# Running log-sum-exp: loads and stores put into the DMA queue in twos instead of by turns

## The chip, the cores and the metric

The kernel runs on one core of a Trainium2 chip. The metric is the device time of one execution in microseconds (us), the median of several runs. The profile is of one execution of its own; its times are counted from the first instruction.

## What is computed

The input is a float32 array of 4 batches, 4096 rows and 4128 columns. For each batch and column the output is the running log-sum-exp down the rows:

```python
out[:, 0, :] = x[:, 0, :]
for t in range(1, S):
    mx = np.maximum(out[:, t - 1, :], x[:, t, :])
    out[:, t, :] = mx + np.log(np.exp(out[:, t - 1, :] - mx) + np.exp(x[:, t, :] - mx))
```

This is the logarithm of the prefix sum of exp(x). Every element is read from HBM once and written back once: 270.5 MB each way.

## The kernel before

**Steps.** A step is 384 rows of one batch, all 4128 columns: 128 partitions with R = 3 neighbouring rows each (6192 KB). 4096 rows make 10 such steps and one of 256 rows (R = 2, 4128 KB). The short step is the first one in batch 0 and the last one in batches 1, 2 and 3. There are 44 steps, numbered 0 to 43 here; the short ones are 0, 21, 32 and 43. One DMA loads a whole step (line L127, `load`), one DMA stores it (L130, `store`). Both are issued on SyncE's queue (SP), which works through its instructions in the order of the program and stops at each until its semaphores allow it. In this text "load n" and "store n" are the transfers of step n.

**Buffers.** The pool `xpool` has 4 buffers of a whole step (`bufs = 4`). exp is written as fp16 into the buffer itself and the logarithm is written back over it as float32, so one buffer holds a step from its load to the end of its store. Load n+4 reuses the buffer of step n and waits until store n has landed (and TensorE has read the buffer).

**Compute.** A step is cut into 4 chunks of 1024 columns (the last one has 1056). For each chunk ScalarE (ACT) takes exp of all rows (L142), TensorE (PE) adds up the rows in PSUM by multiplying with triangular 0/1 matrices, with a carry from the step before (L92, L96), ScalarE takes the logarithm of the first row (L175, `Ln`), TensorE adds the second row, and so on, so a chunk has three stages. The last 32 columns have a PSUM tile of their own (L180). VectorE (DVE) copies the last row's sum into the carry as two fp16 parts (L106, L107).

**Order of the work.** The order is written out by hand (`manual_schedule`). Iteration g of the main loop does the stage of the third row of chunk g-2, of the second row of chunk g-1 and of the first row of chunk g; then exp of chunk g+2; then the matmuls of chunk g+1. ScalarE works strictly in this order. So exp of the first three chunks of step n+1 stands ahead of the last `Ln` of step n: step n can't be finished, and store n not be issued, before load n+1 has landed.

**Order of the transfers.** Loads 0 to 3 are issued at the start. After that a finished step issues its store and then, from the second step on, one load, three steps ahead:

```python
k.t.store()
if bufs <= stored + ahead < len(steps):
    steps[stored + ahead].load()
stored += 1
```

So SP's program is load 0 to 3, store 0, store 1, load 4, store 2, load 5, store 3, load 6, and so on; at the end load 42, store 40, load 43, stores 41, 42, 43. This order is a program order: where `store()` stands in the Python loop fixes what SP has to get past before it, and a store waits for ScalarE's count of the last `Ln` of its own step.

Of the kernel before, what the change touches and what calls it, by code (L numbers as in the profile page):

```python
# [49 lines left out]
def kernel(  # L50
# [23 lines left out]
    bufs = 4  # L74
# [110 lines left out]
    steps = []  # L185
# [9 lines left out]
        assert row == S  # L195

    chunks = [Chunk(s, c) for s in steps for c in range(n_main)]
    ahead = bufs - 1
    for s in steps[:bufs]:
        s.load()  # L200
    stored = 0
    chunks[0].exp()
    chunks[1].exp()
    chunks[0].head()
    for g in range(len(chunks) + R - 1):
        for d in range(R - 1, -1, -1):
            if 0 <= g - d < len(chunks) and d < chunks[g - d].t.r:
                k = chunks[g - d]
                k.stage(d)
                if k.c == last and d + 1 == k.t.r:  # L210
                    k.t.store()
                    if bufs <= stored + ahead < len(steps):
                        steps[stored + ahead].load()
                    stored += 1
        if g + 2 < len(chunks):
            chunks[g + 2].exp()
        if g + 1 < len(chunks):
            chunks[g + 1].head()
# [30 lines left out]
```

## Time and profile before

| | before |
|---|---|
| median of 3 runs | 1262.8 us (1262.75 to 1262.93) |
| span of the profiled execution, first to last instruction | 1261.0 us |
| busy: PE, DVE, ACT | 690.7 (55%), 451.4 (36%), 947.0 us (75%) |
| DMA: bytes, mean rate, mean busy share in the 40 slices | 541.46 MB, 429 GB/s, 90% or more in all but the last |
| transfers on SP's queue | 44 loads and 44 stores |
| load, issue to landing (median) | 42.2 us |
| store, issue to landing (median) | 28.1 us |

The page of the profile lists busy time by engine, then the span in 40 slices, the DMA queues, the chain of work that ended last, and the groups of instructions and of transfers. A transfer is cut over 16 DMA engines, each of which takes its part (8 rows of a step's 128) and then goes on to its part of the next transfer in the queue. A transfer has landed when the last of the 16 has reported. The profiled execution has no time of its own beside the span; the median of the runs is 1.8 us above it, and that is taken as what lies around the span.

### The profile page before, as it was taken

The page shows a single profiled execution, that of the slowest core. Times are in us where ns is not written, and L with a number is a line of the kernel's source. Part 1 is how long each engine was busy: PE and PEld are TensorE (multiplying, and loading weights), DVE is VectorE, ACT ScalarE, POOL GpSimd, SP SyncE. Part 2 cuts the span into 40 slices and gives each one's busy share as a digit, 9 for nine tenths or more (in the row PEclk, how much of TensorE's full clock was granted, in tenths as well). Part 3 has the DMA queues.
Part 4 walks back from the last instruction along what each step waited for, and adds up shares of the span by engine and source line. Part 5 has one row for each costly group of instructions (what it writes and reads, how often), then busy time and mean ns, then how long its engine had stood idle before and what let it go on. Part 6 is the DMA issues. An engine that isn't in the chain of part 4 may idle for free.

```text
span 1261.0 us, 6165 instructions
## 1 busy us (share of the span) xinstructions
PE 690.7 (55%) x2268; PEld 236.3 (19%) x2268; DVE 451.4 (36%) x445; ACT 947.0 (75%) x733; POOL 2.2 (0%) x13
## 2 busy tenths in 40 slices
PE   3666545565565555555346655555534755555562
PEld 1222111121121111111112221211211211111120
DVE  2443333333333333334424333333442433333344
ACT  5997777777777777778569777777866977777784
POOL 0000000000000000000000000000000000000000
PEclk9987787877777777878778777777777778787776
DMA  9999999999999999999999999999999999999998
GB/s 411 411 443 428 432 429 437 431 431 434 437 429 431 431 439 431 434 427 434 436 431 433 434 431 438 430 434 432 435 431 433 437 430 434 433 434 431 433 420 348
DMA packets 12702, 541.46 MB, mean 429 GB/s; under 512 B 1408, under 2 KB 1408, under 8 KB 1408
## 3 DMA queue, kind: packets, MB, share of 16 engines
q1 hardware_dynamic: 12672, 541.07, 99.4%
q8 instruction: 18, 0.29, 0.1%
q14 instruction: 12, 0.10, 0.0%
HBM read 270.53 MB, written 270.53 MB: 429 GB/s over the span
## 4 chain that ended last, share of the span: by engine, by line
DMA 72%; ACT 19%; PE 5%; issue 2%; DVE 1%; SPq 0%; ACTq 0%
DMA xt<-in_x_dram 67%; ACT xt L142 10%; ACT xt L175 9%; DMA out_dram<-xt 5%; PE pt L96 3%; PE pt L92 2%; DVE carry L106 0%; DVE carry L107 0%; ACT xt L180 0%; SPq L130 0%; ACTq L244 0%; SPq L127 0%; ACTq L142 0%; PE qt L92 0%
## 5 line engine op out<-in xcount | busy, mean ns | idle before, releaser
L142 ACT ACTIVATE xt<-xt 128x3072 f16<-128x3072 f32 (+3 forms) x176 | 478.2, 2717 | 247.9 <-DMA xt<-in_x_dram 247.8
L175 ACT ACTIVATE xt<-pt 128x1024 f32<-128x1024 f32 x512 | 487.3, 1029 | 2.5 <-PE pt L96 0.7
L106 DVE CAST carry<-pt 32x1024 f16<-32x1024 f32 x176 | 216.5, 1230 | 760.9 <-ACT xt L175 760.7
L92 PE MATMUL pt<-xt,ident 128*128 128x512 f16 x176 | 76.6, 435 | 493.7 <-ACT xt L175 493.7
L96 PE MATMUL pt<-xt,ident 128*128 128x512 f16 x496 | 203.7, 477 | 35.4 <-ACT xt L175 34.7
L107 DVE TENSOR_TENSOR carry<-pt,carry 32x1024 f16<-32x1024 f32 x176 | 215.8, 1226 | 6.1
L96 PE MATMUL pt<-xt,excl 128*128 128x512 f16 x496 | 187.6, 496 | 0.0
L96 PEld LDWEIGHTS <-ident 128*128 128x128 f16 x496 | 51.0, 103 | 655.0 <-issue 641.3
L92 PE MATMUL pt<-xt,incl 128*128 128x512 f16 x176 | 92.2, 524 | 23.5 <-ACT xt L142 15.1
L92 PE MATMUL pt<-xt,excl 128*128 128x512 f16 x176 | 93.4, 531 | 0.0
L96 PE MATMUL pt<-xt,incl 128*128 128x512 f16 x176 | 92.9, 528 | 0.0
L96 PEld LDWEIGHTS <-excl 128*128 128x128 f16 x536 | 66.6, 124 | 104.1 <-issue 79.5
L92 PE MATMUL pt<-carry,pick 128*128 128x512 f16 x160 | 72.0, 450 | 0.0
L96 PE MATMUL pt<-carry,pick 128*128 128x512 f16 x160 | 68.5, 428 | 0.0
L180 ACT ACTIVATE xt<-qt 128x96 f32<-128x96 f32 (+1 forms) x44 | 10.9, 248 | 46.3 <-PE pt L96 46.3
L92 PEld LDWEIGHTS <-incl 128*128 128x128 f16 x220 | 22.6, 103 | 118.0 <-DVE carry L107 95.3
L92 PEld LDWEIGHTS <-excl 128*128 128x128 f16 x220 | 26.8, 122 | 36.8 <-issue 27.9
L96 PEld LDWEIGHTS <-incl 128*128 128x128 f16 x260 | 27.8, 115 | 10.9 <-issue 4.8
L92 PEld LDWEIGHTS <-pick 128*128 128x128 f16 x200 | 22.9, 114 | 30.4 <-issue 20.4
L96 PEld LDWEIGHTS <-pick 128*128 128x128 f16 x160 | 18.4, 115 | 28.6 <-issue 17.2
L92 PEld LDWEIGHTS <-ident 128*128 128x128 f16 x176 | 19.2, 109 | 22.7 <-issue 12.8
L106 DVE CAST carry_t<-qt 32x32 f16<-32x32 f32 x44 | 8.7, 197 | 26.0 <-ACT xt L180 25.8
(21 smaller groups left out, 56.5 us busy)
## 6 DMA issues: line engine op xcount, KB each, us to landing
xt<-in_x_dram SPq DMA_DIRECT2D x40, 6192.0 KB, 42.2
out_dram<-xt SPq DMA_DIRECT2D x40, 6192.0 KB, 28.1
xt<-in_x_dram SPq DMA_DIRECT2D x4, 4128.0 KB, 37.3
out_dram<-xt SPq DMA_DIRECT2D x4, 4128.0 KB, 29.6
```

The source lines that it names most:

```text
L92: nc.tensor.matmul(pt, lhsT=w, rhs=rhs, start=start, stop=stop, skip_group_check=True)
L96: pe.add_instruction(mybir.InstMatmult(name=nc.get_next_instruction_name(), ins=[pe.lower_ap(rhs), pe.lower_ap(w, for_matmul_weights=True) ...
L106: nc.vector.tensor_copy(cr[HI:HI + 32, :], pt[HI:HI + 32])
L107: nc.vector.tensor_tensor(out=cr[LO:LO + 32, :], in0=pt[HI:HI + 32], in1=cr[HI:HI + 32, :], op=mybir.AluOpType.subtract,)
L142: nc.scalar.activation(self.t.half[:, :, 2 * c0:2 * c0 + w], self.t.xt[:, :, c0:c0 + w], ACT.Exp,)
L175: nc.scalar.activation(t.xt[:, j, c * CH:(c + 1) * CH], pt, ACT.Ln)
L180: nc.scalar.activation(t.xt[:, :, t0:D], self.qt, ACT.Ln)
```

## The change

Steps are no longer stored one at a time. A counter `done` counts finished steps; at every second one (`group = bufs // 2` is 2) the two stores are written into the program, and after them the loads of the two steps that reuse their buffers.

```diff
-    ahead = bufs - 1
+    group = bufs // 2
     for s in steps[:bufs]:
         s.load()
-    stored = 0
+    stored = done = 0
...
                 if k.c == last and d + 1 == k.t.r:
-                    k.t.store()
-                    if bufs <= stored + ahead < len(steps):
-                        steps[stored + ahead].load()
-                    stored += 1
+                    done += 1
+                    if done % group == 0 or done == len(steps):
+                        for s in steps[stored:done]:
+                            s.store()
+                        for s in steps[stored + bufs:done + bufs]:
+                            s.load()
+                        stored = done
```

SP's program becomes load 0 to 3, store 0, store 1, load 4, load 5, store 2, store 3, load 6, load 7, and so on; at the end load 42, load 43, stores 40, 41, 42, 43. The number and size of the transfers, the buffers, and the instruction streams of PE, DVE, ACT and POOL stay as they are. The built programs give each store the same ScalarE count to wait for in both kernels (51 for store 2, 68 for store 3: each waits for its own step alone), and each load the same landed store and the same TensorE count.

## Prediction

> **What bounds the kernel now.** I read the page first, for engines and DMA.
>
> ```profile
> span 1261.0 us, 6165 instructions
> PE 690.7 (55%) x2268; PEld 236.3 (19%) x2268; DVE 451.4 (36%) x445; ACT 947.0 (75%) x733; POOL 2.2 (0%) x13
> DMA  9999999999999999999999999999999999999998
> GB/s 411 411 443 428 432 429 437 431 431 434 437 429 431 431 439 431 434 427 434 436 431 433 434 431 438 430 434 432 435 431 433 437 430 434 433 434 431 433 420 348
> xt<-in_x_dram SPq DMA_DIRECT2D x40, 6192.0 KB, 42.2
> out_dram<-xt SPq DMA_DIRECT2D x40, 6192.0 KB, 28.1
> ```
>
> No compute engine is busy over 75%; the DMA engines are full from end to end at a flat rate. In the trace's packets nearly every one of 49536 bytes takes 1829 ns on its engine, in load and store alike; an engine takes 8 of them per transfer, 14.63 us. With 40 long and 4 short steps (two thirds as long), in and out, that is 2 x 14.63 x (40 + 4 x 2/3) = 1248.5 us per engine; with 1.8 us before the first packet and 0.9 us from last packet to landing, 1251.2 us. The last store lands at 1260.2 us, so only some 9 us are left above the bare engine time. Now where each engine waits:
>
> ```profile
> ACT xt L142 <- DMA xt<-in_x_dram: 247.8, 42, 11.8
> SPq L130 <- ACT xt L175: 1174.4, 44, 30.0
> SPq L127 <- DMA out_dram<-xt: 18.4, 5, 4.9
> ```
>
> ScalarE waits for a load in nearly every step; SP waits for the step's last `Ln` before a store, and hardly ever for a store to land before a load. The chain of waits and SP's timeline show the loop:
>
> ```profile
> 1124.20 42.49 DMA xt<-in_x_dram
> 1166.71 2.76 ACT xt L142
> ...
> 1182.54 0.33 SPq L130
> ```
> ```profile
> 1153.19 0.33 SPq L130 DMA_DIRECT2D out_dram<-xt  x1
> 1153.61 0.38 SPq L127 DMA_DIRECT2D xt<-in_x_dram  x1
> 1182.54 0.33 SPq L130 DMA_DIRECT2D out_dram<-xt  x1
> ```
>
> Load 41 lands at 1166.7, ScalarE starts exp of step 41, and 15.83 us after that start SP issues store 40 (1182.54). This distance is 15.83 us in nearly all long steps. The chain makes it look like a loop of latency, but the 42 us of a load are 28 us of queue and 14.6 us of work: the transfers in front of it keep the engines full. ScalarE's own work for a long step is 23.25 us (1137.36 to 1166.71, less 6.10 us of waiting):
>
> ```profile
> 1137.36 2.76 ACT L142 ACTIVATE xt<-xt 128x3072 f16<-128x3072 f32 x1 [6.16 <-DMA xt<-in_x_dram]
> 1166.71 2.76 ACT L142 ACTIVATE xt<-xt 128x3072 f16<-128x3072 f32 x1 [6.10 <-DMA xt<-in_x_dram]
> ```
>
> against 29.25 us for its two transfers. So the limit is the DMA engines; the question is whether the new order lets them run dry.
>
> **The change, part by part.** Nothing is added or taken away in transfers, bytes or compute. What moves is SP's order.
>
> *Changes of direction.* Before, load and store alternate, so there are about 80 changes; after, half of them. What does one cost? From the landing events (last of 16 engines): load after load at the start 14.60 and 14.62 us apart; load after store 14.55 and store after load 14.69 through most of the run, mean 14.62; the short store 43 after store 42 9.76, against 9.81 for a short store behind a load and 9.68 for a short load behind a store. The two means agree within 0.02 us with unmixed neighbours, and the 0.14 us between load and store comes and goes with the completion. Price of a change of direction 0.00 to 0.02 us; 40 fewer save 0 to 1 us. I take 0.
>
> *Loads later, stores earlier in the queue.* Take four transfers of a pair as 58.5 us, and let load 2m+2 land at 0. Load 2m+3 follows at 14.6, store 2m at 29.3, store 2m+1 at 43.9, load 2m+4 at 58.5. Is each issued in time?
> - Store 2m+1 needs exp of step 2m+2: issued at 0 + 15.83 + 0.35 = 16.2. Its turn comes at 29.3. Margin 13 us.
> - Load 2m+4 stands behind that store on SP and waits for store 2m to land: issued at 29.3 + 0.4 = 29.7. Its turn is at 43.9. Margin 14 us: store 2m+1 runs meanwhile.
> - Load 2m+5 waits for store 2m+1: issued at 44.3, its turn at 58.5. Margin 14 us.
> - Store 2m+2 is behind it on SP. Step 2m+2 is done when ScalarE is 15.83 us into step 2m+3, which it starts at 23.25: 39.1. So it is issued at 44.7, its turn is at 73.1. Margin 28 us.
> - ScalarE needs 46.5 us for two steps of 58.5: it now waits 12 us once a pair for load 2m+4, instead of 6 us twice. Its idle time is moved, not changed.
>
> Each load now has to wait for a landing (before, 5 such waits); what hides that is the store that is still running. The engines don't end together: first and last landing of a transfer are 0.6 us apart at the start, 3.5 us in the middle and 7.6 us for store 41. The foremost engine thus has 14 - 7.6 = 6 us of margin left at worst. If that were gone, it would idle while the last engine, which sets the end, goes on: price 0. So steady state: 0 us.
>
> The Trainium skill speaks against this part: "DMA: Bandwidth & Descriptors", section Rules for kernel authors, says to issue a DMA early and to wait late. By the same page's section on the anatomy of one DMA (told there of GpSimd's path) a transfer that finds no work ahead of it has some 2.0 us of fixed cost; at 20 pairs of loads that would be an estimate of 40 us and about 1303 us in all. The row that decides is the margin above: a load is issued 29 us before it lands instead of 42, and 14 us of that are still queue.
>
> *Start.* Loads 0 to 3, stores 0 and 1 and load 4 are the same. Load 5 is issued after store 1 has landed (83.6) instead of 87.2, behind load 4, which runs until 98.9; store 2 is issued at 86.7 as before, behind load 5. No engine is empty: 0 us.
>
> *End.* Ahead of load 42 stands the same set of transfers, so it lands at 1196.1 as before. Load 43 then goes ahead of store 40 and lands 14.6 us sooner. ScalarE's last wait,
>
> ```profile
> 1220.72 1.91 ACT L142 ACTIVATE xt<-xt 128x2048 f16<-128x2048 f32 x1 [1.34 <-DMA xt<-in_x_dram]
> ```
>
> goes: exp of step 43 starts when ScalarE is free, 1196.13 + 23.26 = 1219.4, 1.3 us sooner, and stores 42 and 43 are issued at about 1233.0 and 1243.5 instead of 1234.33 and 1244.84. Store 41 lands on the last engine at 1235.5 in both, so that engine takes up store 42 without a gap in both. A gain between 0 and 1.3 us, near 0, since the last engine sets the end. I take 0.3.
>
> *Unknown: the hindmost engine.* Its lag grows to 7.6 us by store 41, in jumps and, from 840 us on, by 0.15 us a step in packets of 1844 to 1878 ns instead of 1829. I can't tell whether this depends on order. Bounds: the growth of 2.8 us since 840 us doesn't come, or is doubled: -3 to +3 us. I take 0, as these packets are spread inside the transfer and not at its start.
>
> Sum: 1261.0 - 0.3 = 1260.7 us of span, with the 1.8 us around it **1262.5 us**. By -3 and +3, the forecast's own range is 1259.5 to 1265.5.
>
> **Rivals.**
>
> *The two stores go out together* (slower). If store 2m could go only when step 2m+1 is done, the queue would run dry once a pair: load 2m+2 lands at 0, load 2m+3 at 14.6, the stores come at 16.2, start about 0.6 us later (SP issues load 0 at 1.19, the first packet starts at 1.82), and the next load lands after 16.8 + 3 x 14.63 + 0.9 = 61.6 instead of 58.5: 3.1 us by some 19 pairs is 59 us, and about 10 us more at start (store 0 at 64.0 instead of 37.6) and end: about 1330 us. It decides from the point where a store is issued over 14.6 us after the landing. For it speaks how the Python loop reads; against it, that SP gets to store 2m early and waits there for step 2m's own count (51 against 68). 4%.
>
> *Sixteen engines in one direction are slower* (slower). The two slices that hold only loads show 411 GB/s against 431. Before, first and last engine are 3.5 to 7 us apart, so about two thirds of each 14.6 us are one-way; in pairs of 29.2 us it is 83%. 17% more of the time at 4.6% less is 10 us: 1272 us. It decides if a load behind a load takes over 14.63 us. Against it: 14.60 and 14.62, and the last, one-way store 43 at 9.76; the 411 hold the start-up and one stall of all engines. 7%.
>
> *Changes of direction do cost* (faster). If the 9 us above the bare engine time all came from them, half would go: 1258 us. Against it: the spacings above, and that the long packets lie inside transfers. 6%.
>
> **How the numbers follow.** A difference under 0.2% (2.5 us) is about what a measurement of this kernel can't tell from none. The forecast has 83%, of which 2% fall beyond 0.2% on the fast side and 1% on the slow side. Same: 80%. Faster: 6 + 2 = 8%. Slower: 4 + 7 + 1 = 12%. The range takes the forecast's own, and half a microsecond more towards the slower cases: 1259.5 to 1266.
>
> **What would show it.** DMA slices all 9 but the last; bytes and engine sums as before. Loads' median issue to landing about 29 us instead of 42; stores in two kinds, near 43 us (first of a pair) and 28 us (second). ScalarE's wait for loads again near 248 us, but in about 22 waits of 12 us. SP's waits before loads (L127) for stores to land grow from 5 to nearly 40. SP's timeline shows the first store of a pair issued some 30 us before the second. Wrong, if slices under 9 appear in the middle, if two stores of a pair leave SP within 1 us of each other, or if a pair of steps takes over 58.7 us in steady state.

## The result, and the profile after

The changed kernel takes 1267.32 us (median of 5 runs, 1267.06 to 1268.07) against 1262.93 us before: ratio 1.0037, 95% interval 1.0025 to 1.0049. It is 4.4 us slower, where no difference was forecast, and outside the range given.

The page of the profile after. The lines answer to those of before; in the last two the columns are count, size and median time from issue to landing:

```profile
span 1265.6 us, 6165 instructions
...
PE 660.4 (52%) x2268; PEld 229.4 (18%) x2268; DVE 451.4 (36%) x445; ACT 945.5 (75%) x733; POOL 2.2 (0%) x13
...
DMA  9999999999999999999999999999999999999997
GB/s 409 414 442 428 434 436 429 431 442 424 429 438 429 431 439 429 434 429 438 431 434 429 432 440 429 429 433 437 416 432 427 429 420 440 431 431 439 428 400 339
...
xt<-in_x_dram SPq DMA_DIRECT2D x40, 6192.0 KB, 29.2
out_dram<-xt SPq DMA_DIRECT2D x40, 6192.0 KB, 30.2
```

The DMA engines are full in every slice but the last, and the compute engines do what they did. A load is issued 29 us before it lands, as forecast. So nothing runs dry for long, and yet 4.6 us are lost. The waits, total, times and longest, of all engines and then of SP's queue:

```profile
ACT xt L142 <- DMA xt<-in_x_dram: 259.0, 22, 20.3
```
```profile
SPq L130 <- ACT xt L175: 661.9, 35, 29.9
SPq L127 <- DMA out_dram<-xt: 540.6, 40, 19.6
```

ScalarE waits 22 times instead of 42 for about the same total, and SP waits before each of 40 loads for a store to land. Two of ScalarE's waits and SP's order in between, from the timelines:

```profile
1082.65 2.76 ACT L142 ACTIVATE xt<-xt 128x3072 f16<-128x3072 f32 x1 [13.55 <-DMA xt<-in_x_dram]
...
1141.69 2.76 ACT L142 ACTIVATE xt<-xt 128x3072 f16<-128x3072 f32 x1 [13.05 <-DMA xt<-in_x_dram]
```
```profile
1068.03 0.34 SPq L127 DMA_DIRECT2D xt<-in_x_dram  x1
1068.46 30.38 SPq L130 DMA_DIRECT2D out_dram<-xt  x2
1112.18 15.23 SPq L127 DMA_DIRECT2D xt<-in_x_dram  x2
```

Store 36 leaves SP at 1068.46, store 37 30 us later, the next two loads 15 us apart: the stores are not held for each other. But the pair takes 59.04 us (1082.65 to 1141.69) where 58.5 were forecast. I had named over 58.7 us as a sign that I was wrong.

The landing events show where the time goes. Spacing behind the transfer before, in us, near the end of the run; "middle" is the median of the 16 engines, "last" the one that lands last:

```
              before: store 37, load 40     after: store 36, store 37, load 40, load 41
middle        14.69   14.56                 14.66   14.89   14.49   14.63
last          14.82   14.60                 14.93   14.89   14.60   14.62
```

The foremost engine needs 58.51 us for the pair (first landings of stores 36 and 38, 1104.65 and 1163.16). The middle value jumps where engines change places. One engine is slower, and only in stores. The trace has no engine numbers; an engine is followed by taking, where one packet ends, the packet that starts there. Its packets of one store, in ns, where 1829 is the normal value; each list ends at the last landing:

```
before  store 37: 1844 1829 1829 1878 1872 1853 1844 1872    0.19 us over 8 x 1829
after   store 36: 1852 1872 1853 1858 1881 1862 1853 1900    0.30 us
after   store 37: 1880 1858 1829 1886 1862 1862 1862 1872    0.28 us
after   load 40:  1829 1829 1831 1829 1829 1829 1836 1829    0.01 us
```

This engine loses 0.14 to 0.20 us in most long stores before (median 0.18) and 0.26 to 0.31 us in most after (median 0.28), and next to nothing in loads (median 0.02 us at most). The first three packets of a store, which were nearly spared before, are spared no longer. What else went on then? Busy time by engine (us, with counts) in the stretches of that engine's transfers, before: the first three packets of store 37, the other five, load 40; then after: store 36, store 37, load 40.

```profile
1107.40:1112.90 5.50, 0.33 (x1) 0.10 (x1) 1.23 (x1) 4.96 (x4) 0.00 (x0) 0.62 1.00 432
1112.90:1122.20 9.30, 6.81 (x19) 2.21 (x18) 4.07 (x5) 8.20 (x7) 0.00 (x0) 0.68 0.99 426
1122.20:1136.80 14.60, 7.77 (x36) 2.96 (x35) 4.91 (x4) 8.96 (x8) 0.00 (x0) 0.97 1.00 431
```
```profile
1096.80:1111.60 14.80, 10.73 (x40) 3.75 (x38) 6.97 (x6) 14.47 (x12) 0.00 (x0) 0.83 1.00 430
1111.60:1126.50 14.90, 8.41 (x34) 2.97 (x33) 5.70 (x7) 14.48 (x11) 0.00 (x0) 1.00 1.00 432
1126.50:1141.10 14.60, 4.84 (x18) 1.73 (x18) 2.46 (x2) 2.14 (x3) 0.00 (x0) 0.71 1.00 434
```

The numbers after the length are PE, PEld, DVE, ACT and POOL, then PE's granted clock, the DMA share and GB/s. Before, TensorE paused in each step while ScalarE waited for the load that had just landed, and that pause (0.33 us of work in 5.5) lay on the first three packets of a store. After, ScalarE waits once a pair, while load 2m+4 is still coming, so the pause lies on loads; both stores run beside TensorE from end to end. ScalarE was busy beside the three fast packets (4.96 of 5.50), so it is not the cause by this row; VectorE was not (1.23), so the row leaves it open.

The whole run before says the same: of this engine's packets in long stores, those with TensorE busy for under 5% of their time are 4 ns over 1829 in the mean (88 packets), those with over 95% 35 ns (82). Beside its long stores TensorE is busy for 48% of the time before and 65% after.

From this I formed theory A: while TensorE works, one DMA engine's stores are slowed, and the change moved all stores into that time. Rivals: the order itself costs (B), or ScalarE's or VectorE's accesses do it (A2).

### The profile page after: what moved, and what is told of

It is laid out like the page before. It is cut to its first block, busy times and chain, and to the rows that moved or that the text cites. A ratio compares the mean times of both kernels' runs of the same rounds, so it can differ in the third digit from the quotient of the medians.

```text
span 1265.6 us, 6165 instructions
## 1 busy us (share of the span) xinstructions
PE 660.4 (52%) x2268; PEld 229.4 (18%) x2268; DVE 451.4 (36%) x445; ACT 945.5 (75%) x733; POOL 2.2 (0%) x13
## 4 chain that ended last, share of the span: by engine, by line
DMA 67%; ACT 25%; PE 3%; issue 3%; DVE 0%; SPq 0%; ACTq 0%
DMA out_dram<-xt 40%; DMA xt<-in_x_dram 27%; ACT xt L175 13%; ACT xt L142 12%; PE pt L96 2%; PE pt L92 1%; ACT xt L180 0%; DVE carry L106 0%; DVE carry L107 0%; SPq L127 0%; ACTq L247 0%; ACTq L142 0%; PE qt L92 0%; SPq L130 0%
## 5 line engine op out<-in xcount | busy, mean ns | idle before, releaser
L92 PE MATMUL pt<-xt,ident 128*128 128x512 f16 x176 | 74.4, 422 | 520.9 <-ACT xt L175 520.8
L96 PE MATMUL pt<-xt,ident 128*128 128x512 f16 x496 | 194.1, 454 | 40.6 <-ACT xt L175 40.2
L96 PE MATMUL pt<-xt,excl 128*128 128x512 f16 x496 | 178.8, 476 | 0.0
L92 PE MATMUL pt<-xt,incl 128*128 128x512 f16 x176 | 88.1, 500 | 25.2 <-ACT xt L142 15.0
L96 PE MATMUL pt<-xt,incl 128*128 128x512 f16 x176 | 88.7, 504 | 0.0
L92 PE MATMUL pt<-xt,excl 128*128 128x512 f16 x176 | 88.6, 504 | 0.0
L96 PEld LDWEIGHTS <-excl 128*128 128x128 f16 x536 | 64.4, 120 | 96.0 <-issue 65.9
L92 PE MATMUL pt<-carry,pick 128*128 128x512 f16 x160 | 70.3, 440 | 0.0
L96 PE MATMUL pt<-carry,pick 128*128 128x512 f16 x160 | 67.4, 421 | 0.0
L92 PEld LDWEIGHTS <-excl 128*128 128x128 f16 x220 | 26.1, 119 | 33.9 <-issue 23.0
```

The source lines that it names most:

```text
L92: nc.tensor.matmul(pt, lhsT=w, rhs=rhs, start=start, stop=stop, skip_group_check=True)
L96: pe.add_instruction(mybir.InstMatmult(name=nc.get_next_instruction_name(), ins=[pe.lower_ap(rhs), pe.lower_ap(w, for_matmul_weights=True) ...
```

## The experiments

All times are medians; each is compared with the kernel before on the same chip (1262.72 to 1262.86 us).

**1. Transfers alone, and all but the matmuls.** In the first pair everything but loads and stores is left out, in the second the matmuls alone (`mm` returns at once, and the PSUM tiles are set to 1 once).

```diff
-                k.stage(d)
...
-            chunks[g + 2].exp()
...
-            chunks[g + 1].head()
```
```diff
     def mm(pt, w, rhs, start=False, stop=False):
+        return
```

> Loads and stores by turns as before, with all compute left out (no exp, no matmuls, no logarithm, no carry copies; a store waits for its load alone). Theory A, TensorE's work beside a store slows the store's part on one of the 16 DMA engines: the hindmost engine loses nothing, last store of a long step 14.6 us behind its predecessor in the mean, about 1252 us of span, 1253 to 1255 us of time. Theory B, the order of the transfers itself costs: here the same order as before, so the same drift of some 8 us on the hindmost engine, span about 1260 us.

> Loads and stores in twos, with all compute left out as in the run by turns. Theory A: within 1 us of the run by turns, 1253 to 1255 us. Theory B, a store behind a store or the stores of all engines together cost more: some 4 us slower than the run by turns.

> By turns, all matmuls left out; ScalarE and VectorE do their work as before, on PSUM tiles set to 1 once. Theory A (TensorE): the hindmost engine's stores cost 14.63 us like the others', time 1253 to 1256 us. Theory A2 (ScalarE's or VectorE's accesses slow that engine, not TensorE's): 1261 to 1263 us as with matmuls. Theory B: 1261 to 1263 us.

> In twos, all matmuls left out as in the run by turns. Theory A: within 1 us of the run by turns without matmuls. Theories A2 and B: 3 to 5 us slower than that run, near 1267 us.

| | by turns | in twos |
|---|---|---|
| transfers alone | 1258.29 us | 1257.74 us |
| all but the matmuls | 1259.71 us | 1259.76 us |
| all | 1262.86 us | 1267.32 us |

Without matmuls the order makes no difference to the time (0.05 us), with ScalarE and VectorE at work as before: B is out as what costs the time. In the transfers alone the hindmost engine keeps its distance: its stores from 432 us to the end land 14.63 to 14.71 us apart and its lag stays at 4.6 us by turns. The level was missed: 1258 instead of 1253 to 1255, and 1260 instead of 1253 to 1256 without matmuls, because one engine comes to lag 3.5 to 4.6 us in the first part of the run, without any compute; why, no run shows. Matmuls add 3.1 us by turns and 7.6 us in twos.

A2 is not out: it is a part of the cause. Without matmuls one engine still loses 0.08 us per long store by turns and 0.10 us in twos (medians; at most 0.03 us in the transfers alone). The time doesn't show it, because another engine, some 5 us behind by then, ends last. So ScalarE's or VectorE's work costs that engine something as well; which of the two, no run separates. If the parts add up, which is not shown, matmuls make 0.10 of the 0.18 us before and 0.18 of the 0.28 us after.

**2. TensorE alone beside the transfers.** 3200 matmuls of constant tiles into one PSUM tile, which wait for nothing:

```diff
+    scr = pmain.tile([P, CH], FP32, name="scr")
+    for i in range(3200):
+        mm(scr[:, :MM], incl, carry[i % n_main][:, :MM], start=True, stop=True)
```

> Loads and stores by turns with all compute left out, but TensorE works through 3200 matmuls of constant tiles from the start, waiting for nothing (some 700 to 1370 us, by the granted clock). Theory A (TensorE's work slows one engine's stores, whatever it reads): while TensorE works, all 8 packets of a store on one engine take 1.85 to 1.89 us, 0.25 to 0.35 us a step, and none after its end; 2 to 6 us over the 1258 us without TensorE. Rival (it must read the same buffers, or it is ScalarE's rhythm): 1258 us, no such packets.

> In twos, with the same stream of matmuls. Theory A: the same loss per step as by turns, since TensorE has no pause in either, and a time within 1.5 us of that run. Theory B (the order costs by itself): slower than by turns by 3 us or more.

By turns 1263.01 us, in twos 1263.30 us: 4.7 and 5.6 us more than transfers alone, and the order again makes no difference of note, since TensorE has no pause in either. The matmuls end at some 695 us, so each profile holds both cases. PE's slices by turns, and two stretches in twos:

```profile
PE   9999999999999999999999000000000000000000
```
```profile
560.00:650.00 90.00, 90.00 (x419) 40.81 (x417) 0.00 (x0) 0.00 (x0) 0.00 (x0) 1.00 1.00 434
900.00:1000.00 100.00, 0.00 (x0) 0.00 (x0) 0.00 (x0) 0.00 (x0) 0.00 (x0) 0.50 1.00 431
```

By turns, one engine's packets of store 20 (about 630 us) take 1864 1862 1879 1872 1872 1881 1872 1881 ns, 0.35 us over; those of store 24 (about 750 us) 1829 1829 1829 1829 1833 1834 1834 1844, 0.03 us. The engine's slow packets end with TensorE's work. The matmuls read tiles that no transfer touches, so the same buffer is not needed. Whether weight loads, the tiles read or the sums written to PSUM do it, no run separates.

**3. Less and more of TensorE's work in the kernel in twos.** Less: the sums over a partition's second and third row ahead of the first logarithm are left out, a third of the main matmuls. More: three useless ones for each chunk, which the first real one overwrites.

```diff
-            for j in range(t.r):
+            for j in range(1):
                 for s in range(0, CH, MM):
                     mm(pt[:, s:s + MM], excl if j else incl, ...
```
```diff
+            for i in range(3):
+                mm(pt[:, :MM], incl, self.e(0, 0, MM), start=True)
             for j in range(t.r):
```

> In twos with all compute, but a third of the matmuls of the main tiles left out (the sums over the second and third row of a partition ahead of the first logarithm). Theory A: the loss per store falls from 0.26 us by about a third, 0.06 to 0.1 us a step, 3 to 4 us less time, about 1264 us. Rival (TensorE's amount doesn't matter): 1267 us.

> In twos with all compute, and for each chunk three useless matmuls more, which the first real one overwrites (15 instead of 12). Theory A: the loss per store rises by up to a quarter, 0 to 3 us more time, 1267 to 1270 us. Rival: 1267 us, or more if ScalarE waits longer for TensorE than the 13 us of margin.

| matmuls | TensorE busy beside the engine's long stores | loss per long store of the engine, most of them | time |
|---|---|---|---|
| 1596 (less) | 57% | 0.22 to 0.24 us | 1264.42 us |
| 2268 (as it is) | 65% | 0.26 to 0.31 us | 1267.32 us |
| 2796 (more) | 69% | 0.31 to 0.33 us | 1269.08 us |

The granted clock differed too (0.65, 0.79 and 0.85), so fewer matmuls took longer each. Time follows the amount of TensorE's work, though the DMA engines are the bound and TensorE is idle for over 40% of the span in all three.

**4. Moving TensorE's pause onto the stores.** In steps 4 to 40 ScalarE copies columns onto themselves between a load's landing and the first exp.

```diff
         def exp(self):
             c0, w = self.c * CH, self.w
+            if self.c == 0 and 4 <= steps.index(self.t) <= 40:
+                nc.scalar.activation(self.t.xt[:, 0, :2900], self.t.xt[:, 0, :2900], ACT.Copy)
+                nc.scalar.activation(self.t.xt[:, 1, :2900], self.t.xt[:, 1, :2900], ACT.Copy)
```

> By turns, with all compute; in steps 4 to 40 ScalarE first copies 2900 columns of two rows onto themselves, some 5 us of useless work between the load's landing and the first exp. The copies change no value. TensorE's pause, which lies 1.7 us before to 4.6 us after a load's landing, then reaches some 5 us further into the store that the hindmost engine takes up at that time. Theory A (a store's part on the hindmost engine is slowed while TensorE works, by about 0.03 us per packet of 1.83 us): of 5 slow packets per store 2 to 3 become fast, 0.08 us a step, 2.5 to 3.5 us faster than before, about 1260 us. Rival (it is the order of the transfers, or work in general): same as before, or slower by the added work, 1263 us or more.

> As the run before, with one copy of 2900 columns, some 2.5 us. Theory A: half of its gain, 1.2 to 1.8 us faster than before, about 1261.3 us. Rival: 1263 us.

> In twos, with the same 5 us of copies in steps 4 to 40 (10 us a pair). TensorE's pause then falls on the loads as without them, while the stores run beside its work. Theory A: no gain, within 1 us of the kernel in twos, 1267 us. Rival (more work on ScalarE helps or hurts by itself): moves as the runs by turns do.

> The changed kernel once more, for its time on this chip beside the others and for its profile: 1267 us. If the stops of all engines between 900 and 1040 us of its first profile belong to the kernel they come at the same places again; if they are chance they do not. The hindmost engine's stores again 14.88 to 14.95 us apart.

By turns with 5 us: 1272.23 us, ratio 1.0075 (1.0063 to 1.0088); with 2.5 us: 1265.55 us, 1.0020 (1.0011 to 1.0028). Both are slower, where a gain was expected. Two things were wrong in my expectation. First, a wait doesn't lengthen TensorE's pause, it moves it. In the step whose load lands at 334.1 in both, first before (the pause begins at 331.3), then with the wait:

```profile
338.83 0.59 PE L92 MATMUL pt<-xt,ident 128*128 128x512 f16 x1 [7.50 <-ACT xt L175]
```
```profile
336.66 0.19 PE L96 MATMUL qt<-xt,excl 128*128 128x64 f16 x1
343.95 0.58 PE L92 MATMUL pt<-xt,ident 128*128 128x512 f16 x1 [7.10 <-ACT xt L178]
```

7.1 us instead of 7.5, from 2.8 to 9.9 us after the landing instead of 2.8 us before to 4.7 after. So at best some two microseconds more of a store could be spared, and by the packets none were: where the slow engine can be followed, its long stores cost 0.19 us in the median, with TensorE busy beside them for 46% of the time (before: 0.18 us, 48%). By turns the run therefore doesn't test theory A. Second, the added work ate ScalarE's slack where a short step is near: SP issued the next store 35 us after the last,

```profile
639.91 0.33 SPq L130 DMA_DIRECT2D out_dram<-xt  x1
...
675.51 0.33 SPq L130 DMA_DIRECT2D out_dram<-xt  x1
```

and most engines ran dry. They then started in step (first to last landing 1.5 us instead of 3.1), and load 25, the next one, took 16.1 us on the last engine instead of 14.6. This came back after each such gap (17.0 us for load 22, 16.3 for load 33). In twos with the wait the time is 1267.87 us, no gain, as expected, but by luck: the engine's loss fell from 0.28 to 0.23 us (TensorE busy beside its long stores for 57% instead of 65%), and loads 23 and 37, which took 16.0 and 16.2 us on the last engine instead of 14.6, took the gain back. The changed kernel once more gave 1267.09 us, its long stores again landing 14.89 us behind the transfer before them on the last engine (median).

## Why the prediction was wrong

The queue was predicted rightly, step by step. SP issued store 37 16.3 us after load 38 had landed (forecast 16.2), load 40 0.4 us after store 36 landed, and the two kinds of stores took 43.3 and 28.2 us (forecast 43 and 28). ScalarE lost the wait at step 43 and started 23.14 us after step 42 (1200.74 to 1223.88):

```profile
1223.88 1.92 ACT L142 ACTIVATE xt<-xt 128x2048 f16<-128x2048 f32 x1
```

The price of a change of direction was right as well: with transfers alone half as many changes gave 0.55 us. The Trainium skill's advice that I weighed ("DMA: Bandwidth & Descriptors", section Rules for kernel authors, to issue a DMA early) has no price here that a run shows: with transfers alone loads in twos are issued 28.8 us before they land instead of 43.4, and the time is not longer.

**The step that failed** is the term for the hindmost engine: "I take 0, as these packets are spread inside the transfer and not at its start", with bounds of -3 and +3 us. The row was in the trace of before: packets of 1844 to 1878 ns in stores, none in loads, and the first three of a store nearly spared. I also took the lag for that of one engine. By its packets there are two: one falls 3.3 us behind the foremost by 140 us, in jumps, and stays 3.3 to 4.8 us behind until 1150 us; another loses 0.14 to 0.20 us in most of its long stores from store 2 on and ends last only from store 26 (some 805 us) on. So what I saw from 840 us on had gone on all the time, and 2.8 us was the visible part of some 7.5 us. I asked whether they had to do with the order of transfers, but not what the other engines did beside them, and said of ScalarE's idle time that it "is moved, not changed" as if its place were free. It was the cause: TensorE's pause went with it. The sum by what was measured: 0.10 us more per long store (0.18 to 0.28) x 42.7 stores (40 and 4 of two thirds) = 4.3 us. Most of it goes with the matmuls; 0.02 us of the 0.10 is there without them too (0.08 and 0.10 us).

A second, smaller term: "If that were gone, it would idle while the last engine, which sets the end, goes on: price 0". My margin of 6 us for the foremost engine took transfers of 14.6 us. Around the short step 32 a transfer is 9.7 us and the engines lie 8.7 us apart; load 33 was issued at 900.26, the foremost engine ended load 32 at 900.46, and the first packet of load 33 starts at 900.89. At 915 and 1030 us then all 16 engines, and at 1000 us 7, had packets of 0.2 to 1.5 us over, and loads 33 and 37 came 15.02 and 15.15 us behind their predecessors on the last engine instead of 14.60: 1.0 us. The repeated run has these stops at the same places, the kernel before has none there. TensorE need not be at work: in twos with TensorE alone one comes at 913 to 919 us, long after its last matmul, with the engines 7.7 us apart; in twos without matmuls, with the engines some 4 us apart, there is none. That engines which start in step stop each other is read from these traces and from those with the wait; no run was made for it alone.

Together 5.3 us against 4.6 us between the two last landings (1260.16 and 1264.78). The rest may lie in TensorE's instruction fetches: 18 packets of 16 KB of a queue that the runs without matmuls don't have, each some 1 us on one engine, that hit other engines in each run; that is not shown.

The rivals: the stores did not go out together, and one direction for all engines is not slower (load behind load 14.62 us in twos; the two slices at 411 GB/s that this rival started from also hold the first 6 us of store 0). The 9 us above the bare engine time, which my third rival put down to changes of direction, are by the packets some 7.7 us in the slow engine's stores (0.18 x 42.7) and 1.6 us that all engines lost in the mean at 2 and 54 us, in loads 0 and 3. The other engine's early lag is no part of it, but hides the slow engine where that loses less: the transfers alone by turns land last at 1256.15, 5 us above the bare time, with no slow stores at all. The 3.1 us that matmuls add by turns is therefore less than what they cost the slow engine (0.10 x 42.7 = 4.3 us, if the parts add up).

On one point page and measurement differ. The Trainium skill, "SBUF — State Buffer", section Who interferes with whom, says that DMA never contends with a compute engine. Here matmuls alone, on tiles of their own, made one of 16 DMA engines 2.4% slower in stores (0.35 us of 14.63) and left its loads and the other 15 engines at 0.02 us or less in the median. The measurement decides for the time; whether it happens at SBUF or elsewhere on the way no run here shows.

No run beats the kernel before with all its compute. Its distance to transfers alone is 4.6 us (0.4%). Less work for TensorE, or a longer pause of it beside stores, might take up part of that; by turns no run shows it.

## What to carry to other kernels

Where transfers bound a kernel, its end is set by the slowest single DMA engine: look at the spread between first and last landing and at that engine's packets, not at the mean rate, and follow each engine, since the one that is last early on need not be the one that ends last. A cost on an engine that doesn't end last is hidden from the time, so an unchanged time doesn't clear a suspect. A change that only moves idle time of a compute engine can still cost, if what lay in that time was being spared; before calling a stall "moved for nothing", ask what runs beside its old and its new place. Work out margins for the shortest transfer and the largest spread, not for the typical pair.

## What was not expected of the hardware

- One of 16 DMA engines took 1844 to 1900 ns instead of 1829 per packet of 49536 bytes in stores while TensorE worked; at full TensorE load 0.35 us per store, and next to none in loads. With ScalarE and VectorE at work and no matmuls it was 0.08 to 0.10 us.
- A 5 us wait of ScalarE per step, inside its 6 us of idle time, cost 9.5 us in all, through gaps near the short steps 21 and 32 and long transfers after it.
- With no compute at all, one engine still came to lag 3.5 to 4.6 us in the first part of the run and kept that distance to the end.
